# Storing the two rounded parts of x once and loading them for the gates of a hybrid decoder layer

## The chip, the core and the metric

The kernel runs on one core of one Trainium2 chip. The core has five engines with instruction streams of their own: TensorE (PE, with its weight loads shown apart as PEld), VectorE (DVE), ScalarE (ACT), GpSimd (POOL) and SyncE (SP), which here issues nearly all transfers between the core's SBUF and HBM. The metric is the device time of one launch in microseconds. Lower is better.

## The reference

One layer of a decoder trunk is computed for 2048 prompt tokens and 64 sample tokens (8 sequences of 8), together 2112 tokens of width 1024, in float32. What matters here, cut short:

```python
proj = x @ w_in
(qa, ka, va, za, ba, aa, xb, gb, qc, kc, vc, zc, lc) = jnp.split(proj, SPLIT_POINTS, axis=-1)
# mixer A: conv, silu, l2 norm, chunked gated delta rule over 64 tokens at a time
oa, delta_new = gated_delta_chunked(qa, ka, va, beta, g, st_delta)
oa = head_rms_norm(oa, norm_a_w) * jax.nn.silu(za.reshape(B, T, H_A, DV_A))
# mixer B: a linear recurrence; mixer C: gated linear attention
oc = head_rms_norm(oc, norm_c_w) * jax.nn.silu(zc.reshape(B, T, H_C, DV_C))
x = layer_norm(ALPHA * x + heads @ w_out)
x = layer_norm(ALPHA * x + conv_ffn(x))
```

`za` and `zc` are the gates of mixers A and C, 384 columns each of the one projection `x @ w_in`.

## The kernel before

A float32 product is made of three faster passes. Each operand is split into a rounded part h and a remainder l (ACT rounds, then DVE or POOL subtracts), and the sum is w_h x_h + w_l x_h + w_h x_l. `mm3` (L311) issues the three.

**First stage** (`phase1`). The tokens come in five blocks of 448, 448, 448, 448 and 320. `load_x` (L362 to L374) brings one block of x in four pieces of two 128-row slices of the model width. Each piece lands in one of three staging buffers (`xs`), ACT casts it to `xh` (L370), and DVE subtracts for `xl` (L371). The split blocks stay in SBUF through the stage. Each column tile of the projection (128 columns, `ct`) is 24 matmuls for a block of tokens. The first two column tiles run block by block while x arrives, then the other tiles follow in pairs. ACT's order is the written one in this stage; the other engines' orders come from a scheduler that works with estimates. The gate columns are left out of this stage.

**The stage beside mixer A** (`window_a`). `deltanet` prepares operands for batches of four chunks of 64 tokens (POOL makes M, KD and R; ACT and DVE make decays), solves a triangular system for two batches at a time (the DVE lines L895 and L897), and then runs the recurrence chunk by chunk (PE's `cw`, ACT's copies to X). Beside it runs `gates` (L1071), a generator of 48 dense steps: 16 units (8 blocks of tokens for `za`, then 8 for `zc`) of three column tiles. A step is 24 matmuls into the one PSUM tile `zp` (L1121 to L1123), an ACT copy to `zo` (L1127) and a store (L1128). `deltanet` calls `ahead` and `need` to pull the steps forward, and the scheduler places their instructions between its own. For each unit `gates` loads x anew from the input: four pieces `zx` (L1087) in a staging ring `zs` of two buffers that the weights' pieces `zw` share, each cast by ACT to `xh` (L1088) and subtracted by POOL for `xl` (L1089). The four pieces of the next unit are asked for within the third step of a unit, as PE is done with the old ones.

**Window C** then runs mixer C beside the output projection, and the last stage the feed-forward block, 1519 us from 1520 us to the end, almost all of it matmuls.

Transfers issued by SP are taken in SP's order. An instruction on SP waits there until its buffer is free or its source is ready.

Of the kernel before, what the change touches and what calls it, by code (L numbers as in the profile page):

```python
# [16 lines left out]
T = 2048  # L17
# [17 lines left out]
# ---------------------------------------------------------------- host layout  # L35


def _tiles_of_w_in():
    """Columns of w_in per 128-wide tile, -1 for padding."""
# [60 lines left out]
def _build_consts():  # L100
    """Selectors and masks that follow from the shapes."""
# [33 lines left out]
    # sixteen of each 32 rows are kept; selA and selB take both parts of split rows  # L135
# [4 lines left out]
    # token-major columns: 0-2 -C of head 2p | 3-5 -C of head 2p+1 | 6-11 ln beta  # L140
    # | 12-17 A | 18-23 gl-g+lrk
# [39 lines left out]
def pack(inp):  # L181
    """Lay the inputs out for the chip: permutations, transposes and zero padding only."""
# [84 lines left out]
# ---------------------------------------------------------------- the chip  # L267
# [13 lines left out]
def setup(E, ctx):  # L281
# [3 lines left out]
    E.s = {n: E.dpool.tile(list(sh), F32, name="s_" + n) for n, sh in SCRATCH.items()}  # L285
    E.cols = E.cpool.tile([128, NCOL], F32, name="cols")
# [26 lines left out]
def mm3(nc, ps, wh, wl, xh, xl, first=True, last=True, by_k=False):  # L313
    """float32 product from three single passes over exactly split operands (lists over K)."""
    n = len(wh)
    seq = [(wh, xh), (wl, xh), (wh, xl)]
    order = [(a, k) for k in range(n) for a in range(3)] if by_k else [(a, k) for a in range(3) for k in range(n)]
    for i, (a, k) in enumerate(order):
        w, x = seq[a]
        nc.tensor.matmul(ps, w[k], x[k], start=first and i == 0, stop=last and i == 3 * n - 1)  # L320


def phase1(E):
    nc, tc, s, col = E.nc, E.tc, E.s, E.col
    with ExitStack() as ctx:
# [24 lines left out]
        def first_w():  # L350
            """the first tile in two parts, the second beside the first of the tokens"""
# [32 lines left out]
        def log1p(u, e, t, w):  # L384
            """u = ln(1 + e) for 0 <= e <= 1 with the rounding of 1 + e made good; t, w scratch"""
# [78 lines left out]
        def post_packed():  # L464
            """rates and decays of mixer A, a row for each head and block of tokens"""
# [56 lines left out]
        def conv(ps, nb, key, sst, ocol, taps, bias):  # L522
            """causal width-4 convolution of a block; returns a [128, n] tile"""
# [152 lines left out]
        for i, (ct, nb) in enumerate(seq):  # L676
# [17 lines left out]
            if (ct, nb) == (1, 0):  # L694
                load_w(2)
            if nb < len(NBS) - 1:
# [11 lines left out]
def deltanet(E, ctx, pools, need, ahead):  # L708
    """Gated DeltaNet: chunks of 64 tokens, all six heads. Operands are made for batches of four chunks,
    the triangular systems are solved for two batches at once."""  # L710
# [71 lines left out]
    def shared(g):  # L782
        """per-token columns and chunk decays"""
# [30 lines left out]
    def decay(g, p):  # L814
        """exponents of the decay between tokens of a chunk, masked"""
# [28 lines left out]
    def prep(g):  # L844
        """decays and scores of a batch"""
# [6 lines left out]
    def tokens(g):  # L852
        """keys and values with tokens on the partitions"""
# [25 lines left out]
    def inverse(gs):  # L879
        """U = ((I + L)^-1)^T per chunk and head; 32 x 32 diagonal blocks by substitution, a lane each,  # L880
        and the first product for the block off the diagonal"""
# [30 lines left out]
    def blocks(g):  # L912
        """U of a batch, with its block off the diagonal"""
# [23 lines left out]
    def weights(g):  # L937
        """products of U with the keys"""
# [8 lines left out]
    def outputs(t0):  # L947
        """where the outputs of 128 tokens gather, and their gates"""
# [122 lines left out]
def gates(E, ctx):  # L1071
    """The gates of mixers A and C before their activation; a generator of steps."""
# [4 lines left out]
    op = ctx.enter_context(tc.tile_pool(name="z4", bufs=1))  # L1077
    pm = ctx.enter_context(tc.tile_pool(name="zm", bufs=1, space=PSUM))
    xTv = E.d["xT"].rearrange("(k p) t -> p k t", p=128)
    units = [(nm, nb) for nm in ("za", "zc") for nb in range(len(ZBS))]  # L1080
    W, X = {}, {}

    def split(h, lo, src, name):
        """src from memory into rounded parts"""
        k, n = src.shape[1:]
        st = sp.tile([128, 640], F32, tag="zs", name=name)[:, :k * n].rearrange("p (k t) -> p k t", k=k)
        nc.sync.dma_start(st, src)  # L1087
        nc.scalar.copy(h, st)  # L1088
        nc.gpsimd.tensor_tensor(lo, st, h.bitcast(F32), op=OP.subtract)  # L1089

    def load_w(i):
        h = wp.tile([128, KD, 128], F32R, tag="zh", name=f"zh{i}")
        lo = wp.tile([128, KD, 128], F32R, tag="zl", name=f"zl{i}")
        for j in (0, 4):
            split(h[:, j:j + 4], lo[:, j:j + 4], E.d["w_in"][NT1 + i][:, j:j + 4], f"zw{i}_{j}")
        W[i] = h, lo

    def load_x(u, j):
        if u >= len(units):
            return  # L1100
        t0, n = ZBS[units[u][1]]
        h, lo = (xp.tile([128, 640], F32R, tag=x, name=f"{x}{u}_{j}")[:, :2 * n].rearrange("p (k t) -> p k t", k=2)
                 for x in ("xh", "xl"))
        split(h, lo, xTv[:, 2 * j:2 * j + 2, t0:t0 + n], f"zx{u}_{j}")
        X[u, j] = h, lo

    def steps():
# [4 lines left out]
        for u, (nm, nb) in enumerate(units):  # L1112
            t0, n = ZBS[nb]
            last = u == len(ZBS) - 1
            i0 = 0 if nm == "za" else 3
            for t in range(3):
                ps = pm.tile([128, 320], F32, tag="zp", name=f"zp{u}_{t}")[:, :n]
                wh, wl = W[i0 + t]
# [9 lines left out]
                nc.sync.dma_start(s[nm][t * 128:(t + 1) * 128, t0:t0 + n], o)  # L1128
                if last:
                    load_w(3 + t)  # L1130
                yield
            E.z_done.add((nm, nb))
# [4 lines left out]
def window_a(E):  # L1137
    with ExitStack() as ctx:
# [11 lines left out]
        def need(t0, n):  # L1150
            for nb, (a, w) in enumerate(ZBS):
                while a < t0 + n and t0 < a + w and ("za", nb) not in E.z_done:
# [14 lines left out]
def ln_stats(E, r, m, mv, st):  # L1167
    """mean and variance of the rows of r[:m] to mv[:m]"""
# [6 lines left out]
def ln_scale(E, mv, m):  # L1175
    """variances in mv[:m, ..., 1] to the factors of the layer norm"""
# [18 lines left out]
def head_norm(E, tr, po, z, gain, ones, out):  # L1195
    """out = RMS norm over each head of the rows of po, times silu(z); po and z are overwritten. The gate's
# [775 lines left out]
```

## Time and profile before

| | us |
|---|---|
| median of 3 runs (3035.73 to 3043.57) | 3038.8 |
| span of the profiled execution | 3039.2 |
| TensorE busy in it | 2895.7 |
| first stage, 0 to about 525 | 525 |
| stage beside mixer A, about 525 to 1000 | 475 |
| of it, TensorE busy | 411.3 |

The page gives the busy time of each engine, 40 equal slices of the span, the DMA queues, the chain of work that ended last, and the costliest groups of instructions. In a view of windows each row is a stretch of time with the busy time of PE, PEld, DVE, ACT and POOL (count of instructions in brackets), then the clock that TensorE was granted (1.00 is full), the busy share of the 16 DMA engines, and GB/s. In a view of groups, what stands behind the bar is the idle time of the engine just before those instructions and what ended it.

### The profile page before, as it was taken

The numbers are of one execution on the slowest core, as the hardware profiler recorded it, in microseconds if no ns is written. First come the engines' busy times: TensorE is split into PE (matmuls) and PEld (weight loads), VectorE is DVE, ScalarE is ACT, GpSimd is POOL, SyncE is SP. The second block draws the span as 40 slices with busy tenths as digits, with TensorE's granted clock in tenths as the row PEclk, the third lists the DMA queues.
The fourth block names the chain that finished last, engine by engine and source line by source line (L and its number), as shares of the span: only waits on it lengthen the run. The fifth ranks groups of instructions, "written<-read, shape, count | busy, mean of one in ns | idle before, by whom it ended". The sixth has DMA issues, their size and how long they took to land.

```text
span 3039.2 us, 44833 instructions
## 1 busy us (share of the span) xinstructions
PE 2895.7 (95%) x17755; PEld 2496.9 (82%) x17755; DVE 1597.9 (53%) x2654; ACT 1231.6 (41%) x2591; POOL 843.4 (28%) x892
## 2 busy tenths in 40 slices
PE   8999999789889899998899999999999999999998
PEld 7888789678778677776678888888889999999997
DVE  4564442587665688978533333333366444334446
ACT  4474443446665567756332222222232222222223
POOL 0000001734523545434322222222232222222224
PEclk9999999689898679999999999999999999999999
DMA  6221112433433333322431111111124111111111
GB/s 197 83 74 70 56 61 100 137 106 107 123 99 91 81 120 109 111 82 87 160 123 50 49 42 63 42 56 42 49 104 152 42 47 51 49 42 42 48 43 62
DMA packets 182106, 247.20 MB, mean 81 GB/s; under 512 B 37986, under 2 KB 147640, under 8 KB 181832
## 3 DMA queue, kind: packets, MB, share of 16 engines
q1 hardware_dynamic: 179768, 237.02, 24.2%
q0 software_dynamic: 1984, 7.12, 0.6%
q8 instruction: 140, 2.29, 0.3%
q14 instruction: 70, 0.57, 0.1%
q10 hardware_dynamic: 144, 0.20, 0.0%
HBM read 183.94 MB, written 60.08 MB: 80 GB/s over the span
## 4 chain that ended last, share of the span: by engine, by line
PE 79%; DVE 10%; ACT 4%; issue 3%; DMA 2%; POOL 2%; SPq 0%; POOLq 0%; ACTq 0%; DVEq 0%
PE pm L320 20%; PE pd L320 15%; PE pug L320 15%; PE puv L320 15%; PE s L1364 2%; PE zp L1121 1%; DVE Tm L897 1%; DVE y L1779 1%; DVE tmp L895 1%; DVE K L1337 1%; PE zp L1122 1%; ACT WU L920 1%; PE zp L1123 1%; PE pd L1861 1%; DMA fxl<-s_x1T 1%
## 5 line engine op out<-in xcount | busy, mean ns | idle before, releaser
L1715 DVE SCALAR_TENSOR_TENSOR act<-G,cols,act 128x1024 f32<-128x1024 f32 (+1 forms) x132 | 123.6, 950 | 493.5 <-ACT act L1713 491.1
L1868 DVE TENSOR_TENSOR y<-y,pd 128x512 f32<-128x512 f32 x322 | 220.9, 687 | 203.3 <-PE pd L320 196.8
L1606 POOL TENSOR_TENSOR wl_d<-ws_d,wh_d 128x1024 fp32r<-128x1024 f32 x44 | 106.2, 2415 | 571.3 <-ACT wh_d L1605 547.3
L320 PE MATMUL pd<-wh_d,hh 128*128 128x512 f32 x704 | 215.8, 391 | 4.4 <-DVE y L1868 2.6
L320 PE MATMUL pd<-wh_d,hl 128*128 128x512 f32 x704 | 215.4, 391 | 0.0
L320 PE MATMUL pd<-wl_d,hh 128*128 128x512 f32 x704 | 214.9, 390 | 0.0
L1695 ACT COPY G<-pug 128x512 f32<-128x512 f32 (+2 forms) x110 | 55.2, 503 | 386.3 <-PE pug L320 386.3
L320 PE MATMUL pug<-fxh,wh_g 128*128 128x512 f32 (+2 forms) x880 | 197.0, 352 | 5.3 <-ACT fxh L1658 2.7
L320 PE MATMUL pug<-fxl,wh_g 128*128 128x512 f32 (+2 forms) x880 | 196.6, 352 | 2.5 <-POOL fxl L1659 1.5
L320 PE MATMUL puv<-fxh,wl_v 128*128 128x512 f32 (+2 forms) x880 | 197.1, 353 | 1.1 <-POOL wl_v L1606 1.1
L320 PE MATMUL puv<-fxh,wh_v 128*128 128x512 f32 (+2 forms) x880 | 197.1, 353 | 0.0
L320 PE MATMUL puv<-fxl,wh_v 128*128 128x512 f32 (+2 forms) x880 | 196.9, 352 | 0.0
L320 PE MATMUL pug<-fxh,wl_g 128*128 128x512 f32 (+2 forms) x880 | 196.2, 352 | 0.3 <-POOL wl_g L1606 0.3
L320 PE MATMUL pm<-xh,wh 128*128 128x448 f32 (+1 forms) x800 | 181.9, 360 | 8.3 <-ACT xh L370 6.7
L1605 ACT CAST wh_d<-ws_d 128x1024 fp32r<-128x1024 f32 x44 | 45.7, 1039 | 339.1 <-PE pd L1861 174.9
L320 PE MATMUL pm<-xh,wl 128*128 128x448 f32 (+1 forms) x800 | 181.7, 359 | 0.0
L320 PE MATMUL pm<-xl,wh 128*128 128x448 f32 (+1 forms) x800 | 180.0, 358 | 0.1
L1757 DVE TENSOR_TENSOR hl<-act,hh 128x512 fp32r<-128x512 f32 (+2 forms) x110 | 124.1, 1128 | 99.5 <-ACT hh L1749 99.5
L320 PEld LDWEIGHTS pug<-fxh,wh_g 128*128 128x128 f32 x880 | 156.2, 188 | 21.7 <-ACT fxh L1658 4.3
L320 PEld LDWEIGHTS pug<-fxl,wh_g 128*128 128x128 f32 x880 | 155.7, 188 | 16.9 <-POOL fxl L1659 2.0
L320 PEld LDWEIGHTS puv<-fxh,wl_v 128*128 128x128 f32 x880 | 156.1, 189 | 15.3 <-POOL wl_v L1606 1.3
L320 PEld LDWEIGHTS pm<-xh,wh 128*128 128x128 f32 x800 | 144.6, 188 | 28.9 <-issue 10.1
(731 smaller groups left out, 6371.0 us busy)
## 6 DMA issues: line engine op xcount, KB each, us to landing
ws_d<-in_w_dn SPq DMA_DIRECT2D x44, 512.0 KB
ws_g<-in_w_up SPq DMA_DIRECT2D x43, 512.0 KB
ws_v<-in_w_up SPq DMA_DIRECT2D x43, 512.0 KB
zx<-in_xT SPq DMA_DIRECT2D x56, 256.0 KB
ws<-in_w_in SPq DMA_DIRECT2D x19, 512.0 KB
x<-in_x SPq DMA_DIRECT2D x16, 512.0 KB
s_x<-x SPq DMA_DIRECT2D x16, 512.0 KB
s_x1T<-xt SPq DMA_DIRECT2D x16, 512.0 KB
```

The costliest lines, as they stand in the source:

```text
L320: nc.tensor.matmul(ps, w[k], x[k], start=first and i == 0, stop=last and i == 3 * n - 1)
L895: nc.vector.tensor_tensor(t, Y[:, j + 1:, j:j + 1].to_broadcast([128, k, j + 1]), Tm[:, j:j + 1, :j + 1].to_broadcast([128, k, j + 1]), op ...
L897: nc.vector.tensor_tensor(Tm[:, j + 1:, :j + 1], Tm[:, j + 1:, :j + 1], t, op=OP.subtract)
L920: nc.scalar.copy(o[:, h, :, :, jh * 32:(jh + 1) * 32], Ut[r, :, :3 * mt].rearrange("p i (a c) -> p a c i", a=3)[:, :, g.c0:g.c0 + m])
L1121: nc.tensor.matmul(ps, wh[:, k], xl, start=k == 0, stop=False)
L1364: nc.tensor.matmul(ps[64:, c], K[:, i], Q[:, i], start=True, stop=True)
L1605: nc.scalar.copy(h, t)
L1606: nc.gpsimd.tensor_tensor(lo, t, h.bitcast(F32), op=OP.subtract)
L1695: nc.scalar.copy(G[:, 2 + o:2 + o + m], p[:, :m])
L1715: nc.vector.scalar_tensor_tensor(dst(act), src(i), taps[i], dst(act), op0=OP.mult, op1=OP.add)
L1757: nc.vector.tensor_tensor(dst, act[:, c], hh[:, c].bitcast(F32), op=OP.subtract)
L1868: nc.vector.tensor_tensor(y, y, ps, op=OP.add)
```

## The change

The first stage stores both split parts of x to two scratch tensors in HBM, a block at a time: the program asks for the store of a block's `xh` with column tile 3 and of its `xl` with column tile 4. That is ten stores, 8.65 MB for each part. `gates` then loads `xh` and `xl` from there, straight into the tiles that the matmuls read, in place of loading x, casting it on ACT and subtracting on POOL. The weights of the gates are split as before. A second buffer is given to the copied gates (`zo`). The rest of the diff takes out comments or renames.

```diff
@@ setup
     E.s = {n: E.dpool.tile(list(sh), F32, name="s_" + n) for n, sh in SCRATCH.items()}
+    for n in ("xh", "xl"):
+        E.s[n] = E.dpool.tile([DM, TT], F32, name="s_" + n)
@@ phase1
             if (ct, nb) == (1, 0):
                 load_w(2)
+            if ct in (3, 4):
+                nm, part = (("xh", xh), ("xl", xl))[ct - 3]
+                nc.sync.dma_start(s[nm].rearrange("(k p) t -> p k t", p=128)[:, :, t0:t0 + n], part[nb].bitcast(F32))
@@ gates
-    op = ctx.enter_context(tc.tile_pool(name="z4", bufs=1))
+    op = ctx.enter_context(tc.tile_pool(name="z4", bufs=2))
...
-    def split(h, lo, src, name):
-        k, n = src.shape[1:]
-        st = sp.tile([128, 640], F32, tag="zs", name=name)[:, :k * n].rearrange("p (k t) -> p k t", k=k)
-        nc.sync.dma_start(st, src)
-        nc.scalar.copy(h, st)
-        nc.gpsimd.tensor_tensor(lo, st, h.bitcast(F32), op=OP.subtract)
...
         t0, n = ZBS[units[u][1]]
-        h, lo = (xp.tile([128, 640], F32R, tag=x, name=f"{x}{u}_{j}")[:, :2 * n].rearrange("p (k t) -> p k t", k=2)
-                 for x in ("xh", "xl"))
-        split(h, lo, xTv[:, 2 * j:2 * j + 2, t0:t0 + n], f"zx{u}_{j}")
-        X[u, j] = h, lo
+        both = []
+        for x in ("xh", "xl"):
+            t = xp.tile([128, 640], F32R, tag=x, name=f"{x}{u}_{j}")[:, :2 * n].rearrange("p (k t) -> p k t", k=2)
+            nc.sync.dma_start(t.bitcast(F32), xv[x][:, 2 * j:2 * j + 2, t0:t0 + n])
+            both.append(t)
+        X[u, j] = both
```

How the built programs differ is seen at three places. The first is SP while x arrives in the first stage, from the third piece of the third block of x (`xs_4_281` before, `xs_4_283` now) on. `xs` are pieces of x, `s_gg` are stores of the first column tiles. Before:

```order
L369 DMA xs_4_281<-in_xT 128x2x448
L663 DMA s_gg<-ogb_0_237 128x448
L663 DMA s_gg<-ogb_0_266 128x448
L369 DMA xs_6_285<-in_xT 128x2x448
L369 DMA xs_0_347<-in_xT 128x2x448
L369 DMA xs_2_351<-in_xT 128x2x448
L663 DMA s_gg<-ogb_1_314 128x448
L663 DMA s_gg<-ogb_1_342 128x448
```

Now:

```order
L700 DMA s_xh<-xh_196 128x8x448
L371 DMA xs_4_283<-in_xT 128x2x448
L700 DMA s_xl<-xl_197 128x8x448
L665 DMA s_gg<-ogb_0_239 128x448
L665 DMA s_gg<-ogb_0_268 128x448
L371 DMA xs_6_287<-in_xT 128x2x448
L371 DMA xs_0_349<-in_xT 128x2x448
L371 DMA xs_2_353<-in_xT 128x2x448
L700 DMA s_xh<-xh_273 128x8x448
```

The stores do not stand where the program asks for them but as soon as a block is split: those of blocks 0 to 3, eight in all, stand ahead of the last piece of x (`xs_6_435`), and those of block 4 right behind it.

The second place is POOL at the start of the stage beside mixer A (`xl` and `zl` are remainders of x and of the gates' weights, M, KD, R and rs belong to mixer A). Before:

```order
L810 TENSOR_TENSOR M_4521<-CC_4520,c_mneg 128x256 x3
L856 MEMSET KD_4430 64x384
L857 MEMSET X_4429 64x384
L1089 TENSOR_TENSOR xl_0_4345<-zx_0_4346,xh_0_4344 128x512
L1089 TENSOR_TENSOR xl_1_4351<-zx_1_4352,xh_1_4350 128x512
L859 TENSOR_TENSOR KD_4423<-c_i_4492,eg_4526 64x1536
L830 TENSOR_TENSOR R_4416<-kq_4464,eb_4537 64x256 x2
L830 TENSOR_TENSOR R_4416<-kq_4469,eb_4560 64x256 x2
L1089 TENSOR_TENSOR xl_2_4357<-zx_2_4358,xh_2_4356 128x512
L1089 TENSOR_TENSOR xl_3_4363<-zx_3_4364,xh_3_4362 128x512
```

Now:

```order
L835 TENSOR_TENSOR R_4420<-kq_4468,eb_4541 64x256 x2
L861 MEMSET KD_4434 64x384
L862 MEMSET X_4433 64x384
L835 TENSOR_TENSOR R_4420<-kq_4473,eb_4564 64x256 x2
L1096 TENSOR_TENSOR zl_4373<-zw_0_4374,zh_4372 128x512
L1096 TENSOR_TENSOR zl_4373<-zw_4_4378,zh_4372 128x512
L792 TENSOR_TENSOR rs_4606<-rw_4532,rs_4606 64x256
L864 TENSOR_TENSOR KD_4427<-c_i_4496,eg_4530 64x1536
```

The subtractions for x are gone, and mixer A's instructions and the weights' remainders follow each other directly.

The third place is ACT at the end of that stage, in the recurrence (X, from `cw`) of the last batch before and of the last but one now. `zo` are copies of gates, and `eb`, `ebs`, K, Q and q belong to window C. Before:

```order
L963 COPY X_4422<-cw_9539 64x6x64
L1127 COPY zo_0_8911<-zp_0_8886 128x320
L972 COPY X_4422<-cw_9539 64x6x64
L1127 COPY zo_1_8939<-zp_1_8914 128x320
L963 COPY X_4422<-cw_9560 64x6x64
L1008 COPY X_4429<-cws 64x384
L1127 COPY zo_2_8967<-zp_2_8942 128x320
L1378 ACTIVATE ebs<-b_8_9788 32x8 x4
```

Now:

```order
L977 COPY X_4425<-cw_9041 64x6x64
L1315 ACTIVATE q_1_10792<-b_1_10053 64x256
L968 COPY X_4425<-cw_9078 64x6x64
L1346 COPY K_0_9592<-k_0_9688 32x64
L1351 COPY K_0_9592<-k_0_10061 32x256
L1353 COPY Q_0_9593<-q_0_9690 32x64 x4
L1207 ACTIVATE z_9018<-po_9017 128x384
L977 COPY X_4425<-cw_9078 64x6x64
```

The last gates are copied before the last two batches' recurrence begins, and window C's first instructions stand between its copies.

More of the change, by code (lines that the diff above doesn't have):

```diff
@@ L1076, in gates @@
     sp = ctx.enter_context(tc.tile_pool(name="z3", bufs=2))
-    op = ctx.enter_context(tc.tile_pool(name="z4", bufs=1))
+    op = ctx.enter_context(tc.tile_pool(name="z4", bufs=2))
     pm = ctx.enter_context(tc.tile_pool(name="zm", bufs=1, space=PSUM))
-    xTv = E.d["xT"].rearrange("(k p) t -> p k t", p=128)
-    units = [(nm, nb) for nm in ("za", "zc") for nb in range(len(ZBS))]
+    xv = {n: s[n].rearrange("(k p) t -> p k t", p=128) for n in ("xh", "xl")}
+    units = [(gr, nb) for gr in range(2) for nb in range(len(ZBS))]
     W, X = {}, {}
-    def split(h, lo, src, name):
-        k, n = src.shape[1:]
-        st = sp.tile([128, 640], F32, tag="zs", name=name)[:, :k * n].rearrange("p (k t) -> p k t", k=k)
-        nc.sync.dma_start(st, src)
-        nc.scalar.copy(h, st)
-        nc.gpsimd.tensor_tensor(lo, st, h.bitcast(F32), op=OP.subtract)
     def load_w(i):
@@ L1094, in load_w @@
         for j in (0, 4):
-            split(h[:, j:j + 4], lo[:, j:j + 4], E.d["w_in"][NT1 + i][:, j:j + 4], f"zw{i}_{j}")
+            st = sp.tile([128, 4, 128], F32, tag="zs", name=f"zw{i}_{j}")
+            nc.sync.dma_start(st, E.d["w_in"][NT1 + i][:, j:j + 4])
+            nc.scalar.copy(h[:, j:j + 4], st)
+            nc.gpsimd.tensor_tensor(lo[:, j:j + 4], st, h[:, j:j + 4].bitcast(F32), op=OP.subtract)
         W[i] = h, lo
@@ L1111, in steps @@
         load_w(1), load_w(2)
-        for u, (nm, nb) in enumerate(units):
+        for u, (gr, nb) in enumerate(units):
             t0, n = ZBS[nb]
-            last = u == len(ZBS) - 1
-            i0 = 0 if nm == "za" else 3
+            last = nb == len(ZBS) - 1 and gr < 1
             for t in range(3):
                 ps = pm.tile([128, 320], F32, tag="zp", name=f"zp{u}_{t}")[:, :n]
-                wh, wl = W[i0 + t]
+                wh, wl = W[3 * gr + t]
                 for k in range(KD):
@@ L1127, in steps @@
                 nc.scalar.copy(o, ps)
-                nc.sync.dma_start(s[nm][t * 128:(t + 1) * 128, t0:t0 + n], o)
+                nc.sync.dma_start(s[("za", "zc")[gr]][t * 128:(t + 1) * 128, t0:t0 + n], o)
                 if last:
-                    load_w(3 + t)
+                    load_w(3 * gr + 3 + t)
                 yield
-            E.z_done.add((nm, nb))
+            E.z_done.add((gr, nb))
     return steps()
@@ L1151, in need @@
             for nb, (a, w) in enumerate(ZBS):
-                while a < t0 + n and t0 < a + w and ("za", nb) not in E.z_done:
+                while a < t0 + n and t0 < a + w and (0, nb) not in E.z_done:
                     count[0] += 1
```

## The prediction

> **What bounds the kernel now.** I read the page first, then the two stages that the change touches. The page says that TensorE is the bound nearly everywhere.
>
> ```profile
> span 3039.2 us, 44833 instructions
> PE   8999999789889899998899999999999999999998
> PEclk9999999689898679999999999999999999999999
> PE 79%; DVE 10%; ACT 4%; issue 3%; DMA 2%; POOL 2%; SPq 0%; POOLq 0%; ACTq 0%; DVEq 0%
> ```
>
> Only around the stage beside mixer A (slices 7 to 13) do the busy share and the granted clock fall. So I ask of each part of the change whether TensorE has to wait for it.
>
> First, the arrival of x. In a view of windows of the first stage:
>
> ```profile
> 10.00:20.00 10.00, 8.17 (x36) 6.70 (x35) 5.16 (x15) 5.36 (x10) 0.00 (x0) 1.00 0.96 304
> 20.00:30.00 10.00, 10.00 (x51) 9.22 (x50) 5.39 (x6) 6.34 (x8) 0.00 (x0) 1.00 0.70 229
> 30.00:40.00 10.00, 10.00 (x51) 9.22 (x50) 5.00 (x5) 4.54 (x6) 0.00 (x0) 1.00 0.86 272
> 40.00:50.00 10.00, 10.00 (x51) 9.22 (x50) 4.86 (x6) 5.79 (x9) 0.00 (x0) 1.00 0.63 205
> ```
>
> TensorE never waits after 20 us, but the DMA engines are 63 to 96% busy meanwhile. How close that is, the splits of x show (first and last start behind the durations), beside TensorE's timeline, where the matmuls of 320 columns are the last block of x on the first two column tiles:
>
> ```profile
> L370 ACT CAST xh<-xs x20: 727/940/954, 5.7 to 49.0; 128x896 fp32r<-128x896 f32 x16, 128x640 fp32r<-128x640 f32 x4
> L371 DVE TENSOR_TENSOR xl<-xs,xh x20: 824/1092/1097, 6.6 to 49.8; 128x896 fp32r<-128x896 f32 x16, 128x640 fp32r<-128x640 f32 x4
> 50.67 0.31 PE L320 MATMUL pm<-xh,wh 128*128 128x320 f32 x1
> 57.72 2.81 PE L320 MATMUL pm<-xh,wh 128*128 128x448 f32 x13
> ```
>
> The last piece is split at 49.8 + 0.8 = 50.6 us. The block's 48 matmuls run from 50.67 to 57.72, 0.147 us each. They need the last piece after 18 of them, at 53.3. The whole slack is 2.7 us.
>
> Second, the stage beside mixer A, and the stretch behind it:
>
> ```profile
> 525.00:620.00 95.00, 70.89 (x485) 65.86 (x484) 51.91 (x98) 43.85 (x88) 62.29 (x71) 0.71 0.47 137
> 525.00:1000.00 475.00, 411.27 (x4311) 368.68 (x4309) 305.68 (x594) 269.59 (x609) 206.02 (x243) 0.87 0.38 110
> 1000.00:1060.00 60.00, 51.82 (x392) 38.42 (x390) 43.90 (x109) 36.45 (x118) 36.91 (x66) 0.60 0.30 79
> ```
>
> TensorE idles 475 - 411 = 64 us there. The clock has two levels, as the chain shows by the steps of the same matmuls:
>
> ```profile
> 578.96 0.21 PE zp L1123
> 584.47 0.12 PE zp L1123
> ```
>
> Taken as full and half, a mean of 0.87 means half clock for 26% of the time. At most 64 + 0.26 x 411 / 2 = 117 us could be had in this stage by any change.
>
> **The stores.** A store of one part of a block of 448 tokens is 1024 x 448 x 4 B = 1.835 MB. By the new order eight of them stand ahead of the last piece of x, 14.7 MB. No large store stands in this part of the trace, so I take what the queue carries in the first 60 us, and the fastest of the 40 slices of that time (393 GB/s):
>
> ```profile
> GB/s 0 159 266 346 328 341 338 236 277 288 345 393 246 243 68 317 314 249 91 356 198 345 306 308 276 262 237 281 34 271 199 379 86 0 238 222 10 88 128 243
> q1 hardware_dynamic: 9328, 13.94, 72.2%
> ```
>
> 13.94 MB took 0.722 x 60 us, so 322 GB/s. The eight stores cost 14.7 / 0.322 = 45.6 us by that and 37.4 at 393 GB/s. From the first store (about 14 us) to the last cast at 49 the DMA engines were free for 0.2 + 3.0 + 1.4 + 3.3 = 8 us by the windows above, so the last piece comes 29 to 38 us later, split at 80 to 89 us. Behind it TensorE has 24 matmuls of 0.147 us left (it now interleaves the two column tiles), so the block ends at 83 to 92 instead of 57.7: **25 to 35 us later; I take 30**. Nothing covers this: TensorE takes its instructions in order, and the next column tiles stand behind the block. Nor is it given back, as the rest of the first stage runs TensorE without a gap. The two stores of the last block and a weight tile (0.52 MB, 1.6 us) follow. That tile is needed two times 24 matmuls, 10 us, later and should land in time; without that cover it adds up to 6 us.
>
> By the Trainium skill ("DMA: Bandwidth & Descriptors", "Queues, rings and completion order") descriptors of one queue are consumed in ring order on each engine, so a load behind a store waits for it, as I reckon; no row here shows a load behind so large a store.
>
> The waits may cost clock too. The window 525 to 620 shows 0.71 with TensorE idle a quarter of the time. Stalled blocks hide slower matmuls behind the next wait, all but the last 24 matmuls, which would take 3.5 us more; that is in the range. The skill's "TensorE: Matmul & The Clock Gate", Part 1, says that an idle window of about 3.4 us halves the clock; the trace agrees with two levels.
>
> **The splits beside mixer A.** Taken out are the first two of these groups; the third and fourth stay, and the last row is from the view of waits (total, times, longest):
>
> ```profile
> L1089 POOL TENSOR_TENSOR xl<-zx,xh 128x512 fp32r<-128x512 f32 (+1 forms) x64 | 86.5, 1364 | 132.0 <-ACT xh L1088 110.6 <-issue 17.0 <-DMA kv<-s_v 1.7
> L1088 ACT CAST xh<-zx 128x512 fp32r<-128x512 f32 (+1 forms) x64 | 39.8, 630 | 38.6 <-DMA zx<-in_xT 28.1 <-PE zp L1123 8.6 <-POOL xl L1089 0.9
> L1089 POOL TENSOR_TENSOR zl<-zw,zh 128x512 fp32r<-128x512 f32 x12 | 15.5, 1305 | 19.4 <-ACT zh L1088 17.9 <-issue 1.3
> L1121 PE MATMUL zp<-xl,zh 128*128 128x256 f32 (+1 forms) x384 | 129.0, 336 | 9.5 <-ACT zo L1127 7.2 <-POOL xl L1089 2.3
> DVE ex L822 <- POOL M L810: 25.9, 4, 12.6
> ```
>
> 126 us of work leave, 86.5 on POOL and 39.8 on ACT. But neither bounds the stage (206 and 270 busy of 475), and TensorE itself waited 2.3 us for an x remainder. So the gain is what reaches the chain. At the stage's start it does, as these pieces of the chain in order of time show:
>
> ```profile
> 536.46 2.46 POOL xl L1089 x2
> 544.78 1.27 POOL xl L1089
> 546.07 2.72 DMA zw<-in_w_in
> 549.37 3.08 DMA zw<-in_w_in
> 568.66 1.26 POOL xl L1089
> 576.88 1.24 POOL xl L1089
> ```
>
> Five subtractions, 6.2 us, and two loads of weights, 5.8 us, that waited for the shared staging: 12 us. POOL is busy 62.3 of the first 95 us and keeps M, KD, R and the weights' remainders, which become the late ones: I take 9. Direct waits: 2.3 for xl, and half of the 7.2 for the gates' copy, as ACT has less ahead of it: 6. DVE waited 25.9 us for POOL's M; M mostly waits for ACT's CC behind other copies, so I count a fifth: 5. Behind the stage, 1000 to 1060 holds 51.8 x 0.60 = 31 us of full-clock work in 60; window C's first ACT work now stands earlier: I take 5 of the 29. Against these, the dense steps now end before the last two batches, whose eight chunks then run without them; TensorE waits there for ACT's copies: -7. **Sum: 18 us gained.** The bounds: half of the 117, about 50, is the most I can think of; the loss side is a rival below.
>
> The second buffer of `zo`: in the rows of that tile ACT waited once for its store.
>
> ```profile
>   DMA s_zc<-zo: 1.0, 1
> ```
>
> At most 1 us, counted at nothing, since TensorE's wait is for the one PSUM tile, which stays one.
>
> The loads double: 64 x two parts for 64, 17.3 MB more in 475 us, 54 us of the DMA engines at 322 GB/s. They were busy 0.38 of the time and would be at 0.49: hidden while loads run a unit (three steps, 30 us) ahead.
>
> **Sum.** 3039.2 + 30 - 18 = 3051 us. The span of 3039.2 and the median 3038.8 are 0.4 apart, so nothing is added.
>
> **Rivals.**
>
> 1. *Loads pass the stores.* If the pieces of x keep their place and the stores fill the free time, the first stage loses nothing: 3039 - 18 = 3021, faster. For it: after 60 us the queue has room (the page's DMA row falls from 6 tenths to 2). Against: all are on SP's one queue, eight stores ahead. By the skill's ring order it cannot be.
> 2. *The stage beside mixer A gains more.* If a smoother stage also keeps TensorE's clock up, 45 us of the 117: 3039 + 30 - 45 = 3024, faster. For: clock 0.87, DVE's 25.9 us. Against: only 2.3 us of TensorE's waits name the split.
> 3. *SP becomes the gate.* The eight loads of a unit wait on SP until TensorE frees the old tiles, and the loads of mixer A's k, q and rows queue behind them. Before, the wait there was for POOL's staging. If each of 15 units holds the next prepared batch by one load's time (2.7 to 3.1 us in the chain above), 15 x 3 = 45 us would eat the 18 and more; by a half, as part of it is hidden, 3039 + 30 + 5 = 3074, slower. It decides once the loads are issued less than 3 us before TensorE wants them.
> 4. *Both parts cancel.* 25 lost, 25 gained: 3039.
>
> That the splits stay is excluded by POOL's order.
>
> **How the numbers follow.** Chances: the forecast 0.5, rival 1 0.10, rival 2 0.17, rival 3 0.13, rival 4 0.10. Differences within 0.3% (9 us) are about what a measurement of this kernel cannot tell from no change. The forecast's own range is 3039 + 25 - 25 to 3039 + 35 - 10, 3039 to 3064; of its 0.5 some 0.10 lies within 9 us, rival 2 gives 0.02 to that, and rival 4 all: same 0.22. Faster: 0.10 + 0.15 = 0.25. Slower: 0.40 + 0.13 = 0.53. The range for eight in ten runs from 3016 (30 lost less 50 gained, 3019, or rival 1) to 3078 (rival 3).
>
> **What would show it.** In the changed profile the last cast of `xh` from `xs` should start at 78 to 87 us, the DMA share should stand above 0.9 from 15 to 85 us, and TensorE should idle about 25 us before 90 us. The stage beside mixer A should start near 555 us and last 455 to 465 us, with TensorE's idle time under 55 us, and a gap in its last 40 us. The prediction is wrong in its first step if the last cast still starts near 50 us, and in its second if the stage lasts under 435 us or over 475.

## The result and the profile after

The changed kernel takes 3055.4 us (median of 7 runs, 3044.0 to 3064.7) against 3036.1 (7 runs, 3031.6 to 3043.6): 1.006 times the time before, with a 95% interval of 1.004 to 1.008. It is slower by about 19 us. The profiled execution spans 3058.0 us against 3039.2.

The page of the changed kernel, the same rows as before and the traffic with HBM:

```profile
span 3058.0 us, 44716 instructions
PE   6999999889898979998999999999999999999998
PEclk8999999788998769999999999999999999999999
PE 80%; DVE 9%; DMA 5%; ACT 4%; issue 2%; SPq 1%; POOL 0%; DVEq 0%; ACTq 0%; POOLq 0%
HBM read 201.24 MB, written 77.39 MB: 91 GB/s over the span
```

The first slice of TensorE fell from 8 tenths to 6, its clock with it, and DMA has gone from 2 to 5% of the chain. The loss stands at the very start. In the tile view of the staging buffer `xs` the last cast of `xh` starts at 82.4 us, where it stood at 49.0. The two rows below it, from the same view, give the time that TensorE's weight loads and matmuls were idle for it (before: 8.2 and 6.7 us):

```profile
L372 ACT CAST xh<-xs x20: 724/938/951, 5.3 to 82.4; 128x896 fp32r<-128x896 f32 x16, 128x640 fp32r<-128x640 f32 x4
...
  PEld pm L322: 33.9, 18
  PE pm L322: 27.4, 10
```

Windows of the changed kernel over the arrival of x (columns as before: length, five engines' busy time, then clock, DMA share, GB/s):

```profile
20.00:30.00 10.00, 7.13 (x29) 5.34 (x27) 2.83 (x3) 1.63 (x2) 0.00 (x0) 0.87 1.04 402
30.00:40.00 10.00, 6.65 (x23) 6.00 (x24) 3.19 (x3) 4.86 (x6) 0.00 (x0) 0.62 0.85 286
40.00:50.00 10.00, 5.77 (x27) 4.40 (x25) 1.09 (x1) 1.05 (x2) 0.00 (x0) 0.89 1.04 391
...
70.00:80.00 10.00, 8.22 (x41) 7.04 (x39) 1.31 (x2) 0.72 (x1) 0.00 (x0) 0.91 1.03 363
80.00:90.00 10.00, 6.32 (x24) 6.06 (x24) 0.82 (x1) 2.35 (x4) 0.46 (x1) 0.66 0.77 256
```

The DMA engines run nearly full (the share counts slightly over 1), TensorE waits, and its clock falls to 0.62. The mark for the end of the first stage is here the end of its last matmul of `xh` with `wh` (`pm<-xh,wh`): 558.2 us instead of 525.2, so 33.0 us later. Sixteen more matmuls follow it in both kernels and end 2.3 us after the mark, at 560.5 and 527.5; the expectations of experiments 1, 2, 6 and 7 count from that later point.

The stage beside mixer A is measured here from that mark to the first matmul `ss` of the samples' chunks. The first row is of the kernel before, the second of the changed one:

```profile
525.20:1010.90 485.70, 421.97 (x4431) 378.69 (x4430) 306.43 (x596) 274.71 (x627) 216.54 (x254) 0.86 0.38 109
```

```profile
558.20:1040.50 482.30, 424.00 (x4462) 382.18 (x4461) 287.72 (x620) 243.81 (x584) 143.05 (x206) 0.87 0.49 146
```

POOL lost 73 us of work and ACT 31, yet the stage is only 3.4 us shorter. TensorE's idle time went from 63.7 to 58.3 us. In the view of TensorE's waits a new one leads, and the next is the copy of gates, which was at 7.2:

```profile
PE zp L1123 <- DMA xl<-s_xl: 13.8, 15, 2.3
PE zp L1123 <- ACT zo L1129: 9.2, 7, 4.6
```

At the start of a unit the loads are asked for too late. In the timeline of SP, the first loads of the second unit are issued at 589.46 us, and TensorE starts on them 3.0 us later; it stops again for the second piece, whose load was issued at 590.96. Counted over the 15 later units, TensorE takes the first piece 3.0 to 11.2 us after the issue of its load, and in six of them 3.0 to 3.6 us after it.

```profile
589.46 0.38 SPq L1106 DMA_DIRECT2D xl<-s_xl  x1
...
590.96 0.46 SPq L1106 DMA_DIRECT2D xl<-s_xl  x1
```

```profile
592.46 0.29 PE L1123 MATMUL zp<-xl,zh 128*128 128x256 f32 x1
...
596.21 0.39 PE L1123 MATMUL zp<-xl,zh 128*128 128x256 f32 x1 [2.31 <-DMA xl<-s_xl]
```

From `ss` to the last stage (the matmuls from `pug` to `pd`) the two executions need nearly the same (484.7 and 483.2 us). The last stage itself, which the change doesn't touch, is 9.2 us shorter in the changed kernel's execution. In the kernels of the experiments, none of which touches it, it lasts between 1525 and 1538 us, so I take these 9.2 us as scatter.

### The profile page after: what moved, and what is told of

It is laid out like the page before. It is cut to its first block, busy times and chain, and to the rows that moved or that the text cites. A ratio compares the mean times of both kernels' runs of the same rounds, so it can differ in the third digit from the quotient of the medians.

```text
span 3058.0 us, 44716 instructions
## 1 busy us (share of the span) xinstructions
PE 2903.8 (95%) x17755; PEld 2503.5 (82%) x17755; DVE 1565.2 (51%) x2654; ACT 1194.7 (39%) x2527; POOL 756.2 (25%) x828
## 4 chain that ended last, share of the span: by engine, by line
PE 80%; DVE 9%; DMA 5%; ACT 4%; issue 2%; SPq 1%; POOL 0%; DVEq 0%; ACTq 0%; POOLq 0%
PE pm L322 19%; PE pug L322 15%; PE pd L322 15%; PE puv L322 15%; PE s L1366 2%; DMA xs<-in_xT 2%; PE zp L1123 1%; PE zp L1124 1%; PE zp L1125 1%; DVE y L1781 1%; ACT WU L925 1%; DVE K L1339 1%; PE pw L949 1%; DMA xl<-s_xl 1%; PE cw L967 1%
## 5 line engine op out<-in xcount | busy, mean ns | idle before, releaser
L322 PEld LDWEIGHTS pug<-fxh,wl_g 128*128 128x128 f32 x880 | 156.4, 189 | 14.3 <-POOL wl_g L1608 0.3
```

## The experiments

Each kernel was timed beside the kernel before on the same chip. Where a difference is given in us, it is between those two medians. Ratios carry their 95% intervals. One execution of each kernel was profiled, so stage lengths are of single executions.

**1. The stores later, on ACT.** ACT's order is the written one in the first stage, so a store that ACT issues stays at its column tile.

```diff
-                nc.sync.dma_start(s[nm].rearrange(...)[:, :, t0:t0 + n], part[nb].bitcast(F32))
+                nc.scalar.dma_start(s[nm].rearrange(...)[:, :, t0:t0 + n], part[nb].bitcast(F32))
```

> The ten stores of the rounded parts are issued by ACT, whose order in the first stage is the written one, so they stay at column tiles 3 and 4, behind the last piece of x; all else is as in the changed kernel. Theory 1 (the stores cost only because they stand ahead of x): the last cast of xh from xs starts at 49 to 52 us, the last matmul of the first stage ends near 528 instead of 560.5 us, and the time falls by about 33 us from 3055 to some 3022 us; up to 3031 if the 9 us that came back behind window C were tied to the delay. Theory 2 (17 MB more of traffic cost their time wherever they stand): the first stage still ends at 545 us or later and the time stays at 3045 us or more.

Measured: 3022.4 us against 3038.7, ratio 0.995 (0.994 to 0.996), so faster than the kernel before. Theory 1 holds in the total, to the microsecond by chance. The last cast of the late kernel stands where it was before:

```profile
L372 ACT CAST xh<-xs x20: 727/942/958, 5.7 to 49.3; 128x896 fp32r<-128x896 f32 x16, 128x640 fp32r<-128x640 f32 x4
```

The same bytes cost far less once they no longer stand ahead of x: the first stage ends 4.0 us later than before, at 529.2 us, where theory 1 had next to nothing. What the new gates bring is then seen: about 16 us, with these 4 already taken off.

**2. The stores alone.** The kernel before with the ten stores as the changed kernel has them.

```diff
+            if ct in (3, 4):
+                nm, part = (("xh", xh), ("xl", xl))[ct - 3]
+                nc.sync.dma_start(s[nm].rearrange(...)[:, :, t0:t0 + n], part[nb].bitcast(F32))
```

> The kernel before with the ten stores alone, as the changed kernel asks for them on SP; nobody reads them and the gates load and split x as before. Theory 1 (stores +33 us, gates a gain of a few us beside mixer A, 9 us at random behind): first stage ends at 558 to 562 us, stage beside mixer A lasts 483 us as before, 3036 + 33 = 3069 us. Theory 2 (a part of a delay comes back behind window C whatever its cause): 3060 us. Rival 3 (the new gates gain nothing or lose): 3055 us or less, as the changed kernel.

Measured: 3066.2 us against 3038.7, ratio 1.008 (1.007 to 1.010). The last cast starts almost as late as in the changed kernel:

```profile
L372 ACT CAST xh<-xs x20: 724/937/951, 5.4 to 81.7; 128x896 fp32r<-128x896 f32 x16, 128x640 fp32r<-128x640 f32 x4
```

The first stage ends at 556.2 us, 31.0 later (558.5 by the later point that the expectation counts from), and the stage beside mixer A lasts 489.6 us, 4 longer than before. So the first stage is as theory 1 has it. In the median 27.5 us are lost, between theory 1's 33 and theory 2's 24; the run doesn't settle whether the few us between are scatter. Rival 3's 3055 us or less is not met. By the medians the new gates take some 8 us off the loss (27.5 less 19.3), but the two intervals (1.007 to 1.010 here, 1.004 to 1.008 for the changed kernel) overlap, so these 8 us alone aren't clear of the scatter.

**3. Half of the stores.** Against the kernel of experiment 2, only `xh` is stored.

```diff
-            if ct in (3, 4):
-                nm, part = (("xh", xh), ("xl", xl))[ct - 3]
+            if ct == 3:
+                nm, part = "xh", xh
```

> The kernel before with the stores of xh alone on SP, nobody reads them: four stores, 7.34 MB, stand ahead of the last piece of x. Theory 1 (the loss is the stores' transfer time less the free DMA time of about 8 us): 18.7 to 22.8 less 8, so 11 to 15 us; the last cast of xh from xs starts at 60 to 64 us, the first stage ends at 536 to 540 us, the time is 11 to 15 us over before. Theory 2 (the loss goes with the number of stores that hold up the pieces of x, half of the 31 us that the ten stores alone cost in the first stage): the stage ends near 541 us and the time is 15 us over before.

The first stage ends at 539.3 us, 14.1 later, and the last cast starts at 65.5:

```profile
L372 ACT CAST xh<-xs x20: 724/938/962, 5.8 to 65.5; 128x896 fp32r<-128x896 f32 x16, 128x640 fp32r<-128x640 f32 x4
```

That is inside theory 1 for the end of the stage and 1.5 us over its range for the cast. The two theories are only 1 or 2 us apart at the stage's end, so the end doesn't decide between them. The casts do: they come 16.5 us later with four stores ahead of the last piece and 32.7 with eight, which is one to two, as theory 2 has it, and about 4.1 us for a store. No first 8 us that would be free are seen in them. That the stage's end moves by a little less than half is explained by the 2.7 us of slack between the last split and the matmul that needs it. The total, 3057.5 against 3036.5 us (1.007, 1.005 to 1.009), is 21 us later, over both theories and more than the first stage accounts for. The profiled execution shows 4.5 us of it in the stage beside mixer A (490.2 us). The remainder is not explained.

**4. The stores as early, on another queue.** ACT issues the stores of a block between the casts of the next, and those of the last block behind column tile 1; the rest is the late kernel.

```diff
+        def put(nb, i):
+            t0, n = NBS[nb]
+            nc.scalar.dma_start(s[("xh", "xl")[i]].rearrange(...)[:, :, t0:t0 + n], (xh, xl)[i][nb].bitcast(F32))
...
                 next(beside, None)
+                if nb and k0 in (2, 4):
+                    put(nb - 1, k0 // 2 - 1)
```

> The late kernel with the stores of a block issued by ACT while the next block arrives, so at about the time of the changed kernel's stores, but on ACT's queue; SP's order is that of before. Theory 1 (only the place ahead of x on SP's queue costs): pieces of x pass the stores, the last cast of xh from xs starts at 49 to 55 us, 3022 us. Theory 2 (the DMA engines share their time between the queues, and the bytes cost whatever their queue): the last cast starts at 70 to 85 us, the first stage ends at 547 to 560 us, 3042 to 3055 us.

The last cast starts at 68.6 us, between the 49.3 of the late stores and the 82.4 of stores on SP; the first stage ends at 542.0, 16.8 us later than before, not 33.0. The total is 3033.0 us against 3036.5 (0.999, 0.997 to 1.000), between the two theories. The loads of x and the casts in this kernel:

```profile
L376 SPq DMA_DIRECT2D xs<-in_xT x20: 367/398/1213, 1.7 to 62.5; - x20
L377 ACT CAST xh<-xs x20: 724/938/947, 5.4 to 68.6; 128x896 fp32r<-128x896 f32 x16, 128x640 fp32r<-128x640 f32 x4
```

But the queue isn't all that differs. Each store waits on ACT for a cast of the next block, so when the last load of x is issued at 62.5 us, ACT has issued six stores (the sixth at 54.66 us, the seventh at 63.62), where on SP eight stand ahead of it. At the 4.1 us for a store of experiment 3, six stores on SP would have put the last cast near 74 us (an estimate). So of the 13.8 us between 82.4 and 68.6 some 8 go to the two stores that came later, and at most some 5 to the second queue. Windows of this kernel:

```profile
30.00:40.00 10.00, 10.00 (x43) 9.08 (x42) 3.96 (x4) 4.55 (x6) 0.00 (x0) 0.83 1.05 397
40.00:50.00 10.00, 8.81 (x43) 7.46 (x41) 3.28 (x3) 3.70 (x5) 0.00 (x0) 1.00 1.05 404
50.00:60.00 10.00, 4.40 (x13) 3.88 (x13) 1.50 (x2) 2.32 (x4) 0.00 (x0) 0.72 1.05 399
```

The DMA engines are full at about 400 GB/s, and the changed kernel's fullest window had 402: a second queue adds no bandwidth, and the bytes that are in flight beside x still cost. For the cast that is nearer to theory 2 than to theory 1. The Trainium skill ("DMA: Bandwidth & Descriptors", "Queues, rings and completion order") says that each DMA engine takes turns between the queues that have work for it. The trace fits that, as x gets through while stores are in flight, but with six stores against eight this run can't show its size.

**5. The stores spread out.** One store at each of column tiles 3 to 12, still on ACT.

```diff
-            if ct in (3, 4):
-                nm, part = (("xh", xh), ("xl", xl))[ct - 3]
-                nc.scalar.dma_start(s[nm].rearrange(...)[:, :, t0:t0 + n], part[nb].bitcast(F32))
+            if nb == 0 and 3 <= ct < 13:
+                nm, part = (("xh", xh), ("xl", xl))[(ct - 3) // 5]
+                i = (ct - 3) % 5
+                a, w = NBS[i]
+                nc.scalar.dma_start(s[nm].rearrange(...)[:, :, a:a + w], part[i].bitcast(F32))
```

> As the kernel with late stores, but one store at each of column tiles 3 to 12 in place of five at each of 3 and 4, so that 1.8 MB stand between two weight tiles and not 9.2. In the late kernel TensorE stood 3 us between 160 and 200 us and the first stage ended at 529.2 us, 4.0 later than before. Theory 1 (the crowded stores did that): the stage ends at 525 to 526 us, TensorE is busy 40.0 of 40 us from 160 to 200, and the time is 3017 to 3020 us. Theory 2 (it has another cause): 529 us, and 3022 us.

In the first stage theory 1 holds: it ends at 524.1 us, a little under its range, and from 160 to 200 us TensorE no longer stands still. The late kernel's window, and this one's:

```profile
160.00:200.00 40.00, 37.00 (x168) 31.11 (x167) 23.89 (x45) 29.61 (x48) 1.57 (x5) 0.96 0.52 166
```

```profile
160.00:200.00 40.00, 40.00 (x192) 34.82 (x191) 22.61 (x45) 28.16 (x48) 1.78 (x4) 1.00 0.48 154
```

The total doesn't follow: 3026.9 us against 3034.4 (0.997, 0.996 to 0.999), over the 3017 to 3022 us of the two theories, and a gain of 7.5 us where the late kernel had 16. Its 12 runs lie between 3010.8 and 3041.6 us, a wider scatter than that of the late kernel's six (3019.0 to 3027.1). Why, is open; the last experiments bear on it.

**6. No loads and no splits of x after the first unit.**

```diff
         if u >= len(units):
             return
-        t0, n = ZBS[units[u][1]]
+        t0, n = ZBS[-1]
+        if u > 0:
+            X[u, j] = X[0, j]
+            return
...
```

> The kernel before, with the gates' loads and splits of x left out for all units but the first: the later 15 units multiply the first unit's tiles (which hold the last block of tokens), so the gates are those of wrong tokens. It gives the most that taking the splits away can bring beside mixer A. Theory 1 (the splits never set the pace): the stage from 527.5 us to the last samples' start lasts 476 to 483 us (483.4 before, 480.0 in the changed kernel), the time is 3028 to 3036 us. Theory 2 (they are worth the predicted 18 us, and the late loads of the parts eat it in the changed kernel): the stage lasts 463 to 468 us, the time is near 3018 us.

Measured: 3024.6 us against 3038.7, ratio 0.995 (0.994 to 0.997). The gain of 14 us lies between the two theories' totals. The stage of the profiled execution, the fastest of the six, lasts 478.1 us, 7.6 less than before; counted from 527.5 us as in the expectation it is 475.7, at the lower edge of theory 1 and far from theory 2's 463 to 468. The late kernel, which does load both parts, gained as much in the total. So a gain near the forecast 18 us comes with taking out the splits and their loads, though only half of it is seen in this stage. It is no upper bound, as experiment 9 shows.

**7. One buffer for the copied gates.**

```diff
-    op = ctx.enter_context(tc.tile_pool(name="z4", bufs=2))
+    op = ctx.enter_context(tc.tile_pool(name="z4", bufs=1))
```

> The changed kernel with one buffer for the copied gates, as before. Theory 1 (the second buffer does nothing): 3052 to 3058 us, the stage beside mixer A lasts 478 to 482 us. Rival: the second buffer hides the gates' stores, which queue on SP behind the loads that wait for TensorE; without it the stage lasts 485 us or more and the time is 3061 us or more.

Measured: 3059.0 us against 3038.7, ratio 1.007 (1.005 to 1.009), where the changed kernel had 1.006. That lies between theory 1's 3052 to 3058 us and the rival's 3061, and its interval and the changed kernel's overlap, so the second buffer isn't seen. The profiled execution was the fastest of the six (3047.7 us), and its stage is far shorter than either had it. Its window:

```profile
557.40:1025.00 467.60, 408.92 (x4464) 368.85 (x4462) 286.58 (x620) 243.25 (x584) 143.44 (x206) 0.90 0.50 151
```

TensorE's idle time is 58.7 us, and it was 58.3 in the changed kernel's execution. Yet the stage is 14.7 us shorter, because TensorE's busy time is 15.1 us shorter, at a clock of 0.90 instead of 0.87. And its last stage takes 1534.2 us where the changed kernel's took 1525.2 and the kernel before's 1534.4. As no more than a `zo` buffer differs between the two programs, I take differences of some 10 to 15 us between single executions as scatter of the clock and of that last stage; the six runs of this kernel lie between 3047.7 and 3068.9 us. Two profiles of one kernel, which would show it, were not taken.

**8. Only POOL relieved, only ACT relieved.** Both stand on the spread kernel, with one buffer for the copied gates. The first loads x, casts it on ACT and loads `xl`; the second loads `xh` and x, and POOL subtracts.

```diff
         for x in ("xh", "xl"):
             t = xp.tile(...)
-            nc.sync.dma_start(t.bitcast(F32), xv[x][:, 2 * j:2 * j + 2, t0:t0 + n])
+            if x == "xh":    # the other kernel: if x == "xl"
+                st = sp.tile(...)
+                nc.sync.dma_start(st, xTv[:, 2 * j:2 * j + 2, t0:t0 + n])
+                nc.scalar.copy(t, st)    # the other: nc.gpsimd.tensor_tensor(t, st, both[0].bitcast(F32), op=OP.subtract)
+            else:
+                nc.sync.dma_start(t.bitcast(F32), xv[x][:, 2 * j:2 * j + 2, t0:t0 + n])
...
```

> As the spread kernel (with one buffer for the copied gates, which made no difference), but only xl comes from the scratch tensor; x is loaded and cast to xh on ACT as before. So POOL is rid of its 86.5 us and ACT keeps its 39.8. Theory 1 (the gain comes by way of POOL: the subtractions at the stage's start, the remainders that TensorE waited for, and M; 13 of the predicted 18): 3026 to 3029 us against 3038.7 before and about 3019 for the spread kernel. Theory 2 (the gain comes by way of ACT, which TensorE's waits name most): 3032 to 3037 us.

> The other half: only xh comes from the scratch tensor; x is loaded, and POOL subtracts xh from it for xl as before. ACT is rid of its 39.8 us and POOL keeps its 86.5. Theory 1 (by way of POOL): 3031 to 3036 us, as only the copies of the gates and what POOL waited for ACT's casts gain. Theory 2 (by way of ACT): 3022 to 3027 us.

Measured against 3034.4 us: with POOL relieved 3021.4 us, ratio 0.996 (0.994 to 0.998), with ACT relieved 3033.3, ratio 0.999 (0.998 to 1.000). The gain comes by way of POOL, which is theory 1 in kind: 13 us and 1 us, where it had 10 to 13 and 3 to 8. The two don't add up: the spread kernel, in which both are relieved, gained 7.5 us, and its interval (0.996 to 0.999) overlaps that of POOL alone. Their stages, in the same order:

```profile
523.60:1002.70 479.10, 421.76 (x4451) 380.10 (x4450) 287.22 (x620) 279.63 (x647) 142.68 (x206) 0.87 0.51 147
```

```profile
524.40:1003.40 479.00, 421.22 (x4440) 379.14 (x4439) 301.64 (x600) 239.83 (x565) 224.90 (x264) 0.86 0.51 147
```

One execution of each shows no difference between them, and the one of the kernel with POOL relieved was the slowest of its twelve (3036.4 us). So the difference rests on the twelve runs of each kernel and not on this view.

**9. The loads earlier.** First the order of the two loads, on the spread kernel: the matmuls take `xl` first, so it is loaded first.

```diff
-        for x in ("xh", "xl"):
+        for x in ("xl", "xh"):
...
-        X[u, j] = both
+        X[u, j] = both[::-1]
```

> As the spread kernel, with the load of a piece's xl asked for ahead of its xh, as the matmuls take xl first. TensorE waited 8.7 us for xl in the late kernel. Theory 1 (these waits lie on the path of the stage): they fall below 4 us and the time is 4 to 6 us under the spread kernel. Theory 2 (they only take the place of waits that would come anyway, as the kernel without loads of x was no faster than the late one): within 3 us of the spread kernel.

Measured: 3013.6 us against 3034.4, ratio 0.993 (0.991 to 0.994), 13 us under the spread kernel, timed beside it. The loads' order does count, as theory 1 has it, but the gain is two to three times its 4 to 6 us. TensorE's waits for loads of x in the spread kernel, and then in this one:

```profile
PE zp L1125 <- DMA xl<-s_xl: 8.8, 9, 1.9
...
PE zp L1126 <- DMA xh<-s_xh: 1.5, 3, 0.8
```

```profile
PE zp L1125 <- DMA xl<-s_xl: 4.2, 6, 1.2
PE zp L1126 <- DMA xh<-s_xh: 3.3, 10, 0.8
```

Together they fall by only 2.8 us, so the waits don't explain the 13.

Then a fifth tile of each part, for which blocks of 264 tokens make room, and as a control the same with four tiles:

```diff
-ZBS = [(i * 256, 256) for i in range(7)] + [(1792, 320)]
+ZBS = [(i * 264, 264) for i in range(8)]
...
-    xp = ctx.enter_context(tc.tile_pool(name="z2", bufs=4))
+    xp = ctx.enter_context(tc.tile_pool(name="z2", bufs=5))    # the control: bufs=4
...
-            t = xp.tile([128, 640], F32R, tag=x, ...)
+            t = xp.tile([128, 528], F32R, tag=x, ...)
...
```

> As the kernel with xl asked for first, but with five tiles of each part in place of four, so that the first piece of a unit is loaded ahead of the unit before's last step; to make room for it all eight blocks of gates have 264 tokens (before 256, and 320 the last). Theory 1 (what TensorE still waits for loads, 4.2 and 3.3 us, is on the path): 3 to 7 us under 3013.6 us. Theory 2 (it is not): 3011 to 3017 us.

> The kernel with five tiles of each part, with four again: the eight blocks of 264 tokens stay. It tells which of its two edits brought the 14 us over the kernel with xl asked for first (3013.6 us). Theory 1 (the fifth tile, as the loads then run ahead): 3010 to 3017 us. Theory 2 (the equal blocks, by another order of the dense steps): 2997 to 3003 us.

The kernel with five tiles takes 2999.6 us against 3036.5, ratio 0.988 (0.986 to 0.990): 37 us under the kernel before and the fastest of all. The control takes 3023.2 against 3034.1, ratio 0.997 (0.995 to 0.998). Both miss the ranges of both theories: five tiles gain 14 us on the 3013.6 where at most 7 were expected, and the control is slower than either theory had it. But the two are 24 us apart and their runs don't overlap, so the fifth tile does it and not the equal blocks, which taken alone cost something against 3013.6. With five tiles the first load of the twelfth unit is issued at 759.12 us and TensorE takes it at 796.97, 38 us later:

```profile
759.12 0.42 SPq L1108 DMA_DIRECT2D xl<-s_xl  x1
```

```profile
796.97 0.37 PE L1125 MATMUL zp<-xl,zh 128*128 128x264 f32 x1
```

With four tiles it is 6.3 us for the same unit:

```profile
822.53 0.38 SPq L1108 DMA_DIRECT2D xl<-s_xl  x1
```

```profile
828.87 0.37 PE L1125 MATMUL zp<-xl,zh 128*128 128x264 f32 x1
```

The 38 us are the largest lead of all. Over the units behind the first, the first piece is loaded 15 to 38 us ahead with five tiles and 3 to 17 with four; the other three pieces have no more than 14 us with five tiles.

What the waits for these loads take is small again, 6.4 us with four tiles and 4.3 with five:

```profile
PE zp L1125 <- DMA xl<-s_xl: 3.9, 5, 1.4
PE zp L1126 <- DMA xh<-s_xh: 2.5, 7, 1.0
```

```profile
PE zp L1126 <- DMA xh<-s_xh: 2.6, 3, 1.8
PE zp L1125 <- DMA xl<-s_xl: 1.7, 2, 1.3
```

The stages, with four tiles and with five:

```profile
523.90:1004.70 480.80, 427.23 (x4541) 381.75 (x4540) 297.99 (x656) 258.70 (x641) 144.77 (x218) 0.89 0.50 150
```

```profile
523.80:985.10 461.30, 407.92 (x4475) 369.42 (x4474) 286.70 (x628) 246.23 (x592) 144.59 (x212) 0.89 0.51 153
```

TensorE's idle time is 53.6 and 53.4 us, its busy time 427.2 and 407.9, at the same mean clock. With the fifth tile the dense steps also stand elsewhere: the last ends 376 us into the stage, with four tiles 413. The stage beside mixer A is 19.5 us shorter with five tiles, but the stretch from its end to the last stage is 14.9 us longer (480.0 against 465.1), as the order moved window C's first work across that border; between them 4.6 us are gained. The last stage, which is the same in both, is 8.5 us shorter. That makes 13.1 us between the two profiled spans (3014.5 and 3001.4) and 24 between the medians, of which these single executions explain 5. The profiled execution with four tiles was the fastest of its nine and the one with five the slowest of its four. That the fifth tile brings the gain is shown; by what way is not, as the order of the dense steps changed with it.

## Why the prediction was right, and where not

The forecast was 3051 us, and the changed kernel takes 3055, inside the range and on the likeliest side. The two terms stood up unequally.

**The stores: right.** The last cast was to start at 78 to 87 us and starts at 82.4; the first stage was to end 25 to 35 us later and ends 33.0 later; the stores alone cost 27.5 us in the median. The working was bytes over the queue's rate, less 8 us of free DMA time. For half of the stores it gave 11 to 15 us, and 14.1 were measured in the first stage. But the 8 us as a fixed part are not shown: the casts move by 16.5 and 32.7 us, in proportion to the bytes. Eight stores in 32.7 us are 449 GB/s, more than the 404 of the fullest window here, so some of the bytes did go into free time, but not as a fixed part. The forecast of about 25 us of idle TensorE before 90 us was near: the idle time of the whole first stage rose by 20.8 us (from 8.5 to 29.3), and the other 12 are longer busy time, at a clock of 0.85 over the first 90 us where it was 1.00. I had put the clock at up to 3.5 us and thought most of it hidden behind the waits; it was more, and the idle time somewhat less.

**The DMA share** was 0.9 or more in the windows from 10 to 80 us but for one at 0.85; this was the sign that the transfers, and nothing on TensorE, set the pace.

**The stage beside mixer A: forecast too large, and not by the terms given.** The stage was to be 10 to 20 us shorter; in the profiled execution it was 3.4 shorter, with TensorE idle 58.3 us where under 55 was forecast. In the prediction's measure, 475 us before, that is a stage of 471.6 where 455 to 465 was forecast. By the medians the new gates bring 8 us beside the early stores and 16 with the late ones, against 18 forecast. Of the terms:

- *9 us at the stage's start* is the step that failed most plainly. The five subtractions and the two weight loads left the chain, but the recurrence began 140.4 us into the stage instead of 141.8. The chain showed what ended last, and the next thing behind it was nearly as late. In the changed kernel's chain a store of the first stage and mixer A's own loads (`kv`, `kq`) stand there, 16.4 us in all, which the chain before doesn't have:

```profile
561.74 5.94 DMA s_cv<-ovc
567.75 2.28 DMA kv<-s_k
574.22 2.49 DMA kq<-s_q
592.49 5.70 DMA kq<-s_q
```

 The last of them was issued by SP behind loads of `xh` and `xl`, as the timeline of SP shows (the last `xh` at 591.51, `kq` at 592.02 and 592.49).
- *6 us of direct waits* turned round. The 2.3 us for POOL's remainder became 13.8 for loads, and the wait for the gates' copy rose from 7.2 to 9.2.
- *5 us by way of M* has the right engine: relieving POOL alone gave 13 us, relieving ACT alone about 1. Whether M is the way isn't shown by that. DVE's wait for M fell from 25.9 to 19.1 us:

```profile
DVE ex L827 <- POOL M L815: 19.1, 4, 9.2
```

- *"Hidden while loads run a unit ahead"* was wrong. The loads run no unit ahead: four tiles hold exactly one unit, so a load can start only when TensorE gives its tile back. SP waits for that 26 times:

```profile
SPq L1106 <- PE zp L1125: 20.8, 26, 5.0
```

 This is the place of rival 3. Its condition, loads issued less than 3 us before TensorE wants them, is met at the edge: the second piece of the second unit was wanted at 593.90 us (596.21 less the wait of 2.31), 2.9 us after its issue. Its mechanism shows in the chain above, where a load of `kq` stands behind loads of x, and POOL waits for `kq` two times, 13.0 us. Its price of 45 us isn't reached, as the stage still became 3.4 us shorter. TensorE's direct waits for the two parts were 16.5 us; how much of that is on the path isn't shown.
- *5 us behind the stage*: from `ss` to the last stage 1.5 us were gained (484.7 to 483.2).
- *The second buffer at nothing*: no run shows it to be worth anything.
- *The tail without dense steps, -7 us*: the last 40.5 us of the stage hold 2.1 us of idle time at a clock of 0.80; before, the same stretch had none at about 0.92. The sign is right, the idle time is small.

**The rivals.** Loads didn't pass the stores on one queue; on a second queue the gain from passing was some 5 us at most. Rival 4 (both cancel) had the gain at 25 us, and no run beside the early stores shows more than 8. Rival 2 (a smoother stage keeps the clock up) shows in some kernels that came out shorter, not in all (without loads and splits of x the clock was 0.86): the window of the late kernel shows a clock of 0.89 and TensorE busy 414.7 us instead of 422.0, with only 5 us less idle time:

```profile
529.20:1002.60 473.40, 414.70 (x4463) 371.77 (x4462) 283.00 (x620) 242.07 (x584) 143.75 (x206) 0.89 0.50 149
```

The changed kernel's profiled execution stayed at 0.87 and the one with one `zo` buffer at 0.90. I had priced the stage in waits alone; in these executions much of the difference is in the speed of the matmuls between the waits.

That 33 us lost and 3.4 gained came out near the sum is partly luck. The profiled execution got back 9.2 us in the last stage, where the change does nothing; the medians divide it as 27.5 us lost and 8 gained.

## What to carry to other kernels

Bytes that nobody waits for yet are dear ahead of the loads that feed the first matmuls: look where the scheduler puts a store, not where the program asks for it, and issue it from an engine with a fixed order, where the DMA share is low. When a recomputation is replaced by loads, count how many buffers the loads have: with as many as one unit reads, a load can start only when the unit before gives its buffer back, here as little as 3 us ahead, and one more buffer of each part was worth more (24 us) than all the removed arithmetic (8 to 16). Price a change in a stage with a falling clock by the runs and not by the waits of one execution.

## What the runs showed of the hardware that was not expected

With the same idle time of TensorE (58.3 and 58.7 us) and almost the same program, one execution of the stage took 482.3 us and another 467.6, and the difference is TensorE's busy time, at a granted clock of 0.87 and 0.90. TensorE's busy time in this stage ranged from 407 to 427 us over the kernels tried.

Issuing stores on ACT's queue beside loads on SP's didn't raise the rate (404 GB/s at most, against 402 on one queue), and six stores so issued still delayed the last cast by 19 us (49.3 to 68.6); four on the loads' own queue delayed it by 16 (65.5) and eight by 33 (82.4).

Leaving the loads and the splits of x out altogether (3024.6 us) was slower than loading both parts early enough (2999.6 us), against kernels before of 3038.7 and 3036.5. The order that the scheduler makes of the rest differs between them; which part of it counts, was not tried.
